# Two product matmuls of every seven-product unit issued as two halves of 128 columns

## The chip, the cores and the metric

The kernel runs on one core of a Trainium2 chip. The metric is the device time of one execution in microseconds (us). A profile shows the core's engines: PE (TensorE, matmuls), PEld (TensorE's weight loads, which run beside its matmuls), DVE (VectorE), ACT (ScalarE), POOL (GpSimd) and SP (SyncE, which here only issues DMAs). A matmul streams its moving operand, column by column, through the array that holds its stationary operand; each matmul here has its own weight load.

## What is computed

A decoder layer on x of 512 tokens by 2048 features, in float32. Cut to what matters:

```python
xn = _rmsnorm(x, norm_w)
proj = jnp.einsum('bsd,de->bse', xn, w_in)          # 2048 -> 14352 columns
q, k, v_m, o_m, z_m, i_pre, f_pre, u_g, v_g, z_g = _split_cols(proj)
...
y_m = hm * jax.nn.sigmoid(o_m) * jax.nn.silu(z_m)   # 8 mLSTM heads, chunks of 128 tokens
...
y_g = u * sv.reshape(B, S, D_G) * jax.nn.silu(z_g)  # 8 groups of causal spatial gating
y = jnp.concatenate([y_m, y_g], axis=-1)
h = x + jnp.einsum('bse,ed->bsd', y, w_out)         # 4096 -> 2048
return _rmsnorm(h, final_norm_w)
```

The two large products, with w_in and with w_out, are most of the work.

## The kernel before

**Products of split operands.** Each float32 operand is split into a rounded high part (ACT casts it) and the rest (DVE subtracts): wh and wl of the weights, xah/xal and xbh/xbl of the input, yah/yal and ybh/ybl of y. A product is then three matmuls, high x high, high x low and low x high, accumulated in PSUM. All are in the rounded 32-bit type.

**Seven products instead of eight.** The projection is done in 28 units of 512 columns (`unit_order`, line 36 on). The first is an ordinary product in 512-column matmuls. Each of the other 27 takes a 2 x 2 block product by seven half-size products (`PRODUCTS`, named q1, q6, q2, q7, q5, q4, q3 in this order), of sums of blocks of x (X[j], made at the start) and of w (sums made by an accumulating DMA, line 151, and by DVE, lines 183 and 184). A unit goes over K in 8 chunks (j = 0 to 7). In each chunk the function `products` issues, for each of the seven, two halves of 128 rows (t = 0, 1) with three matmuls each (a = 0, 1, 2) of 128 x 128 by 256 columns: 42 matmuls a chunk, 336 a unit. They accumulate in seven PSUM banks (`product_banks`) and `combine` adds them up after chunk 7. Outside the four units named qk the x part is stationary and w moves; in qk units (`features`) it is the other way round.

**What follows a unit.** Each unit's activations and so on are queued as small pieces in `bg`, and three are run after each chunk of the next unit. Behind a uz unit some of them hold matmuls: the spatial mixing (`mix`, tile mx, line 455, in full float32) and the transposes of y (`turn`, tile ytg, line 473, 128 columns each), which then stand between products in the second and third chunks of the next unit. After the second unit there are four small products (tile rb_ps, line 260).

**The end.** The g half of w_out follows in ordinary 512-column products (og, lines 853 to 855), with the mLSTM heads' work between them (s, nv, ytm). Then 12 blocks of w_out go by seven products again: 4 column blocks (dq) of 6 chunks (g = 0 to 5), tiles q_m, the same function `products`. The last four blocks are ordinary products (fo, lines 917 to 919), and the final norm.

**Order of the work.** PE, DVE and ACT each run their instructions in program order. Weights come in three buffers of wh and wl and four of the raw wf; chunk n's products are issued after the load of chunk n + 4 and the split of chunk n + 2.

Of the kernel before, what the change touches and what calls it, by code (L numbers as in the profile page):

```python
# [16 lines left out]
P = 128  # L17
D = 2048
S = 512
H = 256  # L20
NT = S // P
KT = D // P
NP = KT // 2
# [24 lines left out]
def hybrid_layer(ctx, tc, xs, x, w_first, w_mid, w_gate, w_out, w_last, par, bif, ws_t, sgu, fin_w, out):  # L48
    nc = tc.nc
# [19 lines left out]
    def half(name):  # L69
        return temp(name)[:, 0:S].rearrange("p (a b) -> p a b", a=2)  # L70
# [64 lines left out]
    raws, splits = {}, {}  # L135

    def load(n):
        if n >= NCH or n in raws:
            return
        kind, src = chunks[n]  # L140
        t = wp.tile([P, 5 * H], F32, tag="wf", name=f"wf{n}", bufs=4)
        raws[n] = t
        if kind == "std":
            if n == 0:
                for kk in range(2):
                    nc.sync.dma_start(t[:, kk * S:(kk + 1) * S], src[:, kk * S:(kk + 1) * S])
            else:
                nc.sync.dma_start(t[:, 0:1024], src)
        else:
            nc.sync.dma_start(t, src)  # L150
            nc.gpsimd.dma_start(t[:, 3 * H:5 * H], t[:, H:3 * H], accum_op=ALU.add)  # L151
# [10 lines left out]
    def split(n):  # L162
        if n >= NCH or n in splits:
            return
        kind = chunks[n][0]
        t = raws[n]
        raws[n] = None
        if kind == "std":
            if n >= NF0 + 2:
                h = xb.tile([P, 2, S], F32R, tag="xb", name=f"fh{n}")  # L170
                l = xb.tile([P, 2, S], F32R, tag="xb", name=f"fl{n}")
            else:
                h, l = (wp.tile([P, WS], F32R, tag=tag, name=f"{tag}{n}", bufs=bufs)[
                    :, OFF:OFF + 1024].rearrange("p (a b) -> p a b", a=2) for tag, bufs in (("wh", 3), ("wl", 3)))
            f = t[:, 0:1024].rearrange("p (a b) -> p a b", a=2)
            nc.scalar.copy(h, f)  # L176
            nc.vector.tensor_tensor(l, f, h.bitcast(F32), op=ALU.subtract)  # L177
            splits[n] = (h, l)
            return
        h = wp.tile([P, WS], F32R, tag="wh", name=f"wh{n}", bufs=3)  # L180
        l = wp.tile([P, WS], F32R, tag="wl", name=f"wl{n}", bufs=3)
        e = wp.tile([P, 2 * H], F32, tag="we", name=f"we{n}", bufs=1)
        nc.vector.tensor_tensor(e[:, 0:H], t[:, 3 * H:4 * H], t[:, 2 * H:3 * H], op=ALU.add)  # L183
        nc.vector.tensor_tensor(e[:, H:2 * H], e[:, 0:H], t[:, 0:H], op=ALU.add)  # L184
        for f, c in ((t, slice(0, 5 * H)), (e, slice(5 * H, WS))):
            nc.scalar.copy(h[:, c], f)  # L186
            nc.vector.tensor_tensor(l[:, c], f, h[:, c].bitcast(F32), op=ALU.subtract)  # L187
        splits[n] = tuple(v.rearrange("p (a b) -> p a b", a=7) for v in (h, l))


    xr, X, A21 = {}, {}, {}
# [478 lines left out]
    Y = {}  # L670

    def load_y(kind, g):
        yh, yl = (xb.tile([P, 2, S], F32R, tag="xb", name=f"y{kind}{c}{g}") for c in "hl")
        for f in range(2):
            t = temp(f"yr{kind}{g}_{f}")[:, 0:S]
            nc.sync.dma_start(t, y_dram[(kind, g)][:, f, :])
            nc.scalar.copy(yh[:, f, :], t)
            nc.vector.tensor_tensor(yl[:, f, :], t, yh[:, f, :].bitcast(F32), op=ALU.subtract)
        Y[(kind, g)] = (yh, yl)
# [32 lines left out]
    def run_bg(k):  # L712
        while k > 0 and bg:
            bg.popleft()()
            k -= 1
# [22 lines left out]
    for j in range(NP):  # L738
        n = j
# [13 lines left out]
        wh, wl = splits.pop(n)  # L753
        blocks = ((X[j][0], A21[j]), (X[j][1], X[j][2]))
        if j == 0:
            for kk in range(2):
                for xp, w in ((0, wh), (1, wh), (0, wl)):
                    for q in range(4):
                        cs = slice((q % 2) * P, (q % 2 + 1) * P)
                        nc.tensor.matmul(acc[q], lhsT=blocks[kk][q // 2][xp][:, cs], rhs=w[:, kk, :],  # L760
                                         start=(kk == 0 and xp == 0 and w is wh), stop=False)
# [9 lines left out]
    c0 = [[half(f"e0_{a}{g}") for g in range(2)] for a in range(2)]  # L771
# [9 lines left out]
    def product_banks(un):  # L781
        return {name: (pp if p < 4 else pm).tile([P, S], F32, tag="p" if p < 4 else "m", name=f"{name}_{un}")
                for p, (name, _, _) in enumerate(PRODUCTS)}

    def products(q, xj, wh, wl, opening, closing, features):
        for name, xsl, wsl in PRODUCTS:
            xh, xl = xj[xsl]
            ps = q[name]
            for t in range(2):
                o = ps[:, t * H:(t + 1) * H]  # L790
                cs = slice(t * P, (t + 1) * P)
                first, last = opening and t == 0, closing and t == 1
                if features:
                    ops = ((wh[:, wsl, cs], xh), (wh[:, wsl, cs], xl), (wl[:, wsl, cs], xh))
                else:
                    ops = ((xh[:, cs], wh[:, wsl, :]), (xh[:, cs], wl[:, wsl, :]), (xl[:, cs], wh[:, wsl, :]))
                for a, (st_, mv_) in enumerate(ops):
                    nc.tensor.matmul(o, lhsT=st_, rhs=mv_, start=(first and a == 0), stop=(last and a == 2),  # L798
                                     skip_group_check=True)

    for un in range(1, NA):
        kind, i = order[un]
        q = product_banks(un)
        for j in range(NP):
            n = un * NP + j
            load(n + 4)
            split(n + 2)
            products(q, X[j], *splits.pop(n), j == 0, j == NP - 1, kind == "qk")
            if j == NP - 1:
                c = combine(un, q)  # L810
                AFTER[kind](i, c)
            if un == NA - 1 and j >= 1:
                load_y("g", j - 1)
            run_bg(3)
# [20 lines left out]
    for m, (kind, dq, g) in enumerate(b_chunks):  # L835
        n = NB0 + m
        load(n + 4)
        split(n + 2)
        wh, wl = splits.pop(n)
        if kind == "g":  # L840
            yh, yl = Y[(kind, g)]
            if g == 0:
                acc = [pp.tile([P, S], F32, tag="p", name=f"og{dq}_{q}") for q in range(4)]
                res = []
                for q in range(4):
                    t = temp(f"xr{dq}_{q}")
                    nc.sync.dma_start(t, x[q * P:(q + 1) * P, dq * S:(dq + 1) * S])
                    res.append(t)
            for q in range(4):
                cs = slice(q * P, (q + 1) * P)  # L850
                for kk in range(2):
                    st, sp_ = (g == 0 and kk == 0), (g == NH - 1 and kk == 1)
                    nc.tensor.matmul(acc[q], lhsT=yh[:, kk, cs], rhs=wh[:, kk, :], start=st, stop=False)  # L853
                    nc.tensor.matmul(acc[q], lhsT=yh[:, kk, cs], rhs=wl[:, kk, :], start=False, stop=False)  # L854
                    nc.tensor.matmul(acc[q], lhsT=yl[:, kk, cs], rhs=wh[:, kk, :], start=False, stop=sp_)  # L855
                if g == NH - 1:
                    t = res[q]
                    nc.vector.tensor_tensor(t, t, acc[q], op=ALU.add)
                    nc.sync.dma_start(acc_dram[:, q, dq * S:(dq + 1) * S], t)
            run_bg(6)  # L860
            if dq == 3:
                flush(("m", g))
                if g < 6:
                    sums_y(g)
                else:
                    load_y("m", g)
        else:
            if g == 0:
                q = product_banks(f"m{dq}")
                res = {}  # L870
                for a in range(2):
                    for b in range(2):
                        t = half(f"xc{dq}_{a}{b}")
                        nc.sync.dma_start(t, block(acc_dram, a, b, dq))
                        res[(a, b)] = t
            products(q, Y[("m", g)], wh, wl, g == 0, g == 5, False)
            if g == 5:
                c = combine(f"m{dq}", q)
                for a in range(2):
                    for b in range(2):  # L880
                        t = res[(a, b)]
                        nc.vector.tensor_tensor(t, t, c[a][b], op=ALU.add)
                        if dq < 3:
                            nc.sync.dma_start(block(acc_dram, a, b, dq), t)
                        else:
                            for k in range(2):
                                xacc[(2 * a + k, dq, b)] = t[:, k, :]
    for tt in range(NT):
        for dq in range(3):
            t = row(f"xacc{tt}_{dq}")[:, 0:S]  # L890
# [8 lines left out]
    for a in range(4):  # L899
        t = temp(f"fw{a}")  # L900
# [4 lines left out]
    for tt in range(NT):  # L905
# [4 lines left out]
        for dq in range(4):  # L910
            ps = pp.tile([P, S], F32, tag="p", name=f"fo{tt}_{dq}")
# [110 lines left out]
```

## Time and profile before

| | us |
|---|---|
| median of 3 runs | 1561.7 |
| the three runs | 1553.22, 1561.70, 1561.98 |
| the profiled execution | 1571.57 |
| its span, first to last instruction | 1569.9 |

| stretch of the span | us | what runs |
|---|---|---|
| first unit | 0 to 60 | 512-column products, split of x |
| 27 seven-product units | 60 to 1153 | 9,072 matmuls at line 798 |
| g half of w_out, mLSTM heads | 1153 to 1395 | 512-column products |
| seven products of w_out | 1395 to 1514 | 1,008 matmuls at line 798 |
| last blocks, final norm | 1516 to 1570 | 512-column products |

In the timeline of PE a row gives the start and the length in us, the engine, line, operation, output and inputs, the size, how many were merged, and behind it the idle time before it with what ended it. Matmuls overlap: one is 0.28 us long from its start to its modelled end, but the next starts some 0.115 us after it. The distance from start to start is what one costs, and the length is not. In a row of a wait or of the windows x144 means that 144 instructions touch the stretch.

### The profile page before, as it was taken

The page shows a single profiled execution, that of the slowest core. Times are in us where ns is not written, and L with a number is a line of the kernel's source. Part 1 is how long each engine was busy: PE and PEld are TensorE (multiplying, and loading weights), DVE is VectorE, ACT ScalarE, POOL GpSimd, SP SyncE. Part 2 cuts the span into 40 slices and gives each one's busy share as a digit, 9 for nine tenths or more (in the row PEclk, how much of TensorE's full clock was granted, in tenths as well). Part 3 has the DMA queues.
Part 4 walks back from the last instruction along what each step waited for, and adds up shares of the span by engine and source line. Part 5 has one row for each costly group of instructions (what it writes and reads, how often), then busy time and mean ns, then how long its engine had stood idle before and what let it go on. Part 6 is the DMA issues. An engine that isn't in the chain of part 4 may idle for free. (4 is left out here: it accounts for less than half of the span.)

```text
span 1569.9 us, 30095 instructions
## 1 busy us (share of the span) xinstructions
PE 1545.9 (98%) x11864; PEld 1485.4 (95%) x11864; DVE 1183.7 (75%) x1944; ACT 874.6 (56%) x1340; POOL 285.3 (18%) x384
## 2 busy tenths in 40 slices
PE   9999999999999999999999999999999999999997
PEld 7899999999999999999999999999988788889986
DVE  8787767877966876976877977678887665697875
ACT  6665455654654555554655565454776666553333
POOL 1411112211122211121211111111202222011100
PEclk9999999999999999999999999999999999999999
DMA  9777878787788777778787777877964665798962
GB/s 319 210 192 187 228 177 209 185 202 193 213 203 215 188 211 184 210 190 214 192 211 186 200 203 199 212 201 196 277 195 156 206 226 188 238 265 238 277 231 107
DMA packets 118510, 326.99 MB, mean 208 GB/s; under 512 B 13534, under 2 KB 20702, under 8 KB 118369
## 3 DMA queue, kind: packets, MB, share of 16 engines
q1 hardware_dynamic: 77456, 243.30, 48.1%
q0 software_dynamic: 40192, 80.66, 26.7%
q8 instruction: 93, 1.52, 0.4%
q10 hardware_dynamic: 720, 1.11, 0.2%
q14 instruction: 49, 0.39, 0.1%
HBM read 229.37 MB, written 32.74 MB: 167 GB/s over the span
## 5 line engine op out<-in xcount | busy, mean ns | idle before, releaser
L186 ACT CAST wh<-wf 128x1280 fp32r<-128x1280 f32 x240 | 301.9, 1264 | 379.9 <-issue 237.8
L187 DVE TENSOR_TENSOR wl<-wf,wh 128x1280 fp32r<-128x1280 f32 x240 | 356.7, 1488 | 174.3 <-ACT wh L186 174.0
L798 PE MATMUL q<-wh,xbh 128*128 128x256 f32 x1472 | 413.7, 281 | 1.4 <-ACT e L774 1.4
L798 PE MATMUL q<-wl,xbh 128*128 128x256 f32 x1472 | 412.9, 281 | 1.2 <-DVE wl L187 1.2
L798 PE MATMUL q<-wh,xbl 128*128 128x256 f32 x1472 | 412.7, 280 | 0.0
L151 POOL DMA_DIRECT2D wf<-wf x240 | 205.3, 857 | 1010.9 <-DMA wf<-w_mid 243.2
L798 PE MATMUL q<-wh,xah 128*128 128x256 f32 x1104 | 311.8, 282 | 0.0
L798 PE MATMUL q<-wl,xah 128*128 128x256 f32 x1104 | 309.5, 280 | 0.0
L798 PE MATMUL q<-wh,xal 128*128 128x256 f32 x1104 | 309.4, 280 | 0.0
L798 PEld LDWEIGHTS q<-wh,xbh 128*128 128x128 f32 x1472 | 281.1, 191 | 1.8 <-ACT e L774 1.6
L798 PEld LDWEIGHTS q<-wl,xbh 128*128 128x128 f32 x1472 | 276.9, 188 | 1.9 <-DVE wl L187 1.8
L798 PEld LDWEIGHTS q<-wh,xbl 128*128 128x128 f32 x1472 | 276.3, 188 | 0.0
L798 PEld LDWEIGHTS q<-wh,xah 128*128 128x128 f32 x1104 | 210.8, 191 | 0.7 <-ACT e L774 0.2
L798 PEld LDWEIGHTS q<-wl,xah 128*128 128x128 f32 x1104 | 207.7, 188 | 0.1
L798 PEld LDWEIGHTS q<-wh,xal 128*128 128x128 f32 x1104 | 207.2, 188 | 0.0
L186 ACT CAST wh<-we 128x512 fp32r<-128x512 f32 x240 | 148.2, 618 | 89.6 <-DVE we L184 89.2
L187 DVE TENSOR_TENSOR wl<-we,wh 128x512 fp32r<-128x512 f32 x240 | 164.7, 686 | 17.2 <-ACT wh L186 17.2
L183 DVE TENSOR_TENSOR we<-wf 128x256 f32<-128x256 f32 x240 | 101.4, 422 | 20.0 <-issue 9.0
L184 DVE TENSOR_TENSOR we<-we,wf 128x256 f32<-128x256 f32 x240 | 101.4, 423 | 5.4
L853 PE MATMUL og<-wh,ygh 128*128 128x512 f32 x256 | 100.9, 396 | 1.6 <-ACT wh L176 1.6
L854 PE MATMUL og<-wl,ygh 128*128 128x512 f32 x256 | 101.5, 397 | 0.1
L855 PE MATMUL og<-wh,ygl 128*128 128x512 f32 x256 | 101.3, 396 | 0.0
(284 smaller groups left out, 2865.9 us busy)
## 6 DMA issues: line engine op xcount, KB each, us to landing
wf<-w_mid SPq DMA_DIRECT2D x216, 640.0 KB, 4.7
wf<-wf POOLq DMA_DIRECT2D x240, 256.0 KB, 5.2
wf<-w_out_p SPq DMA_DIRECT2D x40, 512.0 KB, 4.1
wf<-w_last SPq DMA_DIRECT2D x24, 640.0 KB, 5.7
xr<-xs SPq DMA_DIRECT2D x16, 256.0 KB, 6.1
xt<-x SPq DMA_DIRECT2D x8, 512.0 KB, 7.5
ozd<-e SPq DMA_DIRECT2D x16, 256.0 KB, 2.6
ygd<-yfg SPq DMA_DIRECT2D x16, 256.0 KB, 4.5
```

The source lines that it names most:

```text
L151: nc.gpsimd.dma_start(t[:, 3 * H:5 * H], t[:, H:3 * H], accum_op=ALU.add)
L183: nc.vector.tensor_tensor(e[:, 0:H], t[:, 3 * H:4 * H], t[:, 2 * H:3 * H], op=ALU.add)
L184: nc.vector.tensor_tensor(e[:, H:2 * H], e[:, 0:H], t[:, 0:H], op=ALU.add)
L186: nc.scalar.copy(h[:, c], f)
L187: nc.vector.tensor_tensor(l[:, c], f, h[:, c].bitcast(F32), op=ALU.subtract)
L798: nc.tensor.matmul(o, lhsT=st_, rhs=mv_, start=(first and a == 0), stop=(last and a == 2), skip_group_check=True)
L853: nc.tensor.matmul(acc[q], lhsT=yh[:, kk, cs], rhs=wh[:, kk, :], start=st, stop=False)
L854: nc.tensor.matmul(acc[q], lhsT=yh[:, kk, cs], rhs=wl[:, kk, :], start=False, stop=False)
L855: nc.tensor.matmul(acc[q], lhsT=yl[:, kk, cs], rhs=wh[:, kk, :], start=False, stop=sp_)
```

## The change

`products` takes one more argument, `cut`, the name of a product with t and a. The one matmul that it names is issued as two matmuls of 128 columns with the same stationary operand, into the two halves of the same 256 PSUM columns. In the 27 units that is in the first chunk (j = 0) the first of the last three matmuls (q3, t = 1, a = 0), and in the fifth (j = 4) the fourth (q1, t = 1, a = 0); in the last stage the fourth of the second and the fourth chunk of each column block (g = 1 and 3). What is computed stays the same.

```diff
-    def products(q, xj, wh, wl, opening, closing, features):
+    def products(q, xj, wh, wl, opening, closing, features, cut=None):
         for name, xsl, wsl in PRODUCTS:
             xh, xl = xj[xsl]
             ps = q[name]
             for t in range(2):
-                o = ps[:, t * H:(t + 1) * H]
                 cs = slice(t * P, (t + 1) * P)
...
                 for a, (st_, mv_) in enumerate(ops):
-                    nc.tensor.matmul(o, lhsT=st_, rhs=mv_, start=(first and a == 0), stop=(last and a == 2),
-                                     skip_group_check=True)
+                    parts = (0, P, H) if (name, t, a) == cut else (0, H)
+                    for c0, c1 in zip(parts, parts[1:]):
+                        nc.tensor.matmul(ps[:, t * H + c0:t * H + c1], lhsT=st_, rhs=mv_[:, c0:c1],
+                                         start=(first and a == 0), stop=(last and a == 2), skip_group_check=True)
...
-            products(q, X[j], *splits.pop(n), j == 0, j == NP - 1, kind == "qk")
+            cut = {0: ("q3", 1, 0), 4: ("q1", 1, 0)}.get(j)
+            products(q, X[j], *splits.pop(n), j == 0, j == NP - 1, kind == "qk", cut)
...
-            products(q, Y[("m", g)], wh, wl, g == 0, g == 5, False)
+            products(q, Y[("m", g)], wh, wl, g == 0, g == 5, False, ("q1", 1, 0) if g in (1, 3) else None)
```

On the other engines the instructions and their order stay. On PE, the end of the first chunk of the second unit before (q_1_763 is q3's bank, wh_617 and wl_618 the weights, xbh_302 and xbl_303 the x part; x2 means two alike):

```order
L798 MATMUL q_1_763<-wh_617,xbh_302 128x256
L798 MATMUL q_1_763<-wl_618,xbh_302 128x256
L798 MATMUL q_1_763<-wh_617,xbl_303 128x256
L798 MATMUL q_1_763<-wh_617,xbh_302 128x256
L798 MATMUL q_1_763<-wl_618,xbh_302 128x256
L798 MATMUL q_1_763<-wh_617,xbl_303 128x256
L260 MATMUL rb_ps<-diag,ones 128x128 x2
```

The same place now:

```order
L799 MATMUL q_1_763<-wh_617,xbh_302 128x256
L799 MATMUL q_1_763<-wl_618,xbh_302 128x256
L799 MATMUL q_1_763<-wh_617,xbl_303 128x256
L799 MATMUL q_1_763<-wh_617,xbh_302 128x128 x2
L799 MATMUL q_1_763<-wl_618,xbh_302 128x256
L799 MATMUL q_1_763<-wh_617,xbl_303 128x256
L260 MATMUL rb_ps<-diag,ones 128x128 x4
```

The fourth matmul has become two of 128 columns. The four small products behind it now stand together, where they were parted by three products of the next chunk.

## The prediction

> **What bounds the kernel now.** I read the page first, then the PE waits, then the PE timeline matmul by matmul, because a PE that is busy all the time can still run at different paces.
>
> ```profile
> span 1569.9 us, 30095 instructions
> PE 1545.9 (98%) x11864; PEld 1485.4 (95%) x11864; DVE 1183.7 (75%) x1944; ACT 874.6 (56%) x1340; POOL 285.3 (18%) x384
> ...
> PE ytm L473 <- DVE oz L639: 2.5, 1, 2.5
> ```
>
> PE is busy for 98% of the span, and the longest single wait of PE on anything is 2.5 us. So time can hardly be won by hiding something; it is the spacing of the matmuls that counts. Of the 11,864 matmul records 10,080 are the products at L798 (27 units of 8 chunks of 42, and 4 of 6 chunks of 42). The spacing comes from the timeline: the first and last row of two stretches without interruption, 172 records and 153 records.
>
> ```profile
> 309.80 0.28 PE L798 MATMUL q<-wh,xbl 128*128 128x256 f32 x1
> ...
> 329.94 0.28 PE L798 MATMUL q<-wh,xal 128*128 128x256 f32 x1
> ...
> 388.75 0.28 PE L798 MATMUL q<-wh,xah 128*128 128x256 f32 x1
> ...
> 405.97 0.28 PE L798 MATMUL q<-wh,xbl 128*128 128x256 f32 x1
> ```
>
> 171 steps in 20.14 us are 117.8 ns each; 152 steps in 17.22 us are 113.3 ns. The same instruction on the same shapes has two paces, 4.5 ns apart, and each pace lasts for hundreds of matmuls. Whole units show it too (columns: stretch, its length, then busy time and count of PE, PEld, DVE, ACT, POOL, clock, DMA share, GB/s):
>
> ```profile
> 388.40:426.96 38.56, 38.37 (x338) 38.17 (x337) 36.67 (x60) 21.53 (x26) 6.41 (x9) 1.00 0.79 214
> 548.01:587.59 39.58, 39.58 (x339) 39.58 (x338) 28.49 (x42) 23.41 (x29) 7.65 (x9) 1.00 0.80 207
> 1073.62:1112.19 38.57, 38.38 (x338) 38.18 (x337) 36.15 (x58) 21.53 (x26) 6.32 (x8) 1.00 0.77 211
> 1450.00:1490.00 40.00, 40.00 (x342) 39.98 (x341) 34.12 (x53) 15.52 (x18) 7.59 (x9) 1.00 0.96 265
> ```
>
> The first and third line are the only two units that run nearly whole at the fast pace; the second is an ordinary one at the slow pace. The granted clock is 1.00 in all, so it is no clock state. Following the timeline through all units, I count about 1,070 fast products, nearly all in these two units, the beginning of the units behind them, and short pieces of some 43 matmuls in four others. About 9,000 are slow. If all became fast, 9,000 x 4.5 ns = 40 us would go.
>
> What switches the pace? Interruptions of the stream:
>
> ```profile
> 152.09 0.28 PE L798 MATMUL q<-wh,xbl 128*128 128x256 f32 x1
> 152.56 1.03 PE L455 MATMUL mx<-e,ws 128*128 128x256 f32 x4
> 154.13 0.28 PE L798 MATMUL q<-wh,xbh 128*128 128x256 f32 x1
> ...
> 155.95 0.28 PE L798 MATMUL q<-wl,xbh 128*128 128x256 f32 x1
> ...
> 159.10 0.60 PE L473 MATMUL ytg<-ident,e 128*128 128x128 f32 x4
> 160.12 0.28 PE L798 MATMUL q<-wh,xal 128*128 128x256 f32 x1
> 160.80 0.28 PE L798 MATMUL q<-wh,xbl 128*128 128x256 f32 x1
> 161.14 0.66 PE L473 MATMUL ytg<-ident,e 128*128 128x128 f32 x4
> 161.76 0.28 PE L798 MATMUL q<-wl,xah 128*128 128x256 f32 x1
> 162.93 0.28 PE L798 MATMUL q<-wh,xbl 128*128 128x256 f32 x1
> ```
>
> Before the mixing products (mx) the pace is slow; after them it is fast (154.13 to 155.95, 16 steps, 114 ns), still fast after the first transposes (160.12 to 160.80, 6 steps, 113 ns), and slow after the second (161.76 to 162.93, 10 steps, 117 ns), where it stays to the next interruption. The same sequence repeats behind four other uz units. So the pace is a lock between the stream of weight loads and the stream of matmuls; a disturbance shifts one against the other, and they settle again in one lock or the other.
>
> **The change, part by part.** It removes nothing and moves no work between engines; 62 matmuls (27 units x 2, 4 x 2 in the last stage) become two halves each, so PE and PEld get 62 instructions more. Each pair is a disturbance in the sense above, one every 168 matmuls.
>
> *Price of a cut.* No row shows such a half. Nearest are the transposes, 128 columns each with a weight load of their own:
>
> ```profile
> L473 PE MATMUL ytg<-ident,e 128*128 128x128 f32 x64 | 10.0, 279 | 0.4
> L260 PE MATMUL rb_ps<-diag,ones 128*128 128x128 f32 x8 | 1.3, 287 | 0.2 <-DVE diag L259 0.2
> ```
>
> Four of them take 0.60 us from the first start to the last end (159.10); less the 0.28 us of the last, three steps are 0.32 us, 108 ns a step, though half the columns are streamed. A pair then costs 216 ns where one matmul cost 113 or 118: +100 ns. Settling again, as behind the interruptions above, I put at 10 to 15 ns. So 62 x 0.115 = +7.1 us, all on the path, because PE has no slack. The bounds: at the low end a half streams in half of 113 ns and its load hides, +0. At the high end a half runs like the plain f32 matmuls of rb_ps, whose four matmuls leave eight records, two passes of about 110 ns each: a pair 440 ns, +330 ns, 62 x 0.33 = +20 us. The operands here are the rounded type of the products, which pass once, and the transposes pass once too; so I take +7.1.
>
> The Trainium skill, "TensorE: Matmul & The Clock Gate", speaks against the change in "LDWEIGHTS (loading the stationary operand)": a load takes its 128 columns over 1.2, 106.7 ns, whatever the matmul streams. By it the estimate for a pair is 213 ns, +100 over a fast product, 62 x 0.10 = 6.2 us; the transposes' 108 ns agree.
>
> *Which lock follows a cut.* This decides, and no row shows it. For fast: all ten mixings outside the qk units were followed by the fast pace, and in two of four cases the mere change from a qk unit to the next one. For slow: the second transposes, five times of five. Of the kinds of disturbance in these units somewhat over half end fast. A cut has one advantage over the others: its geometry is always the same, without a wait on another engine, so from the fast lock it gives always the same answer. If that answer is "fast", the fast lock absorbs: once in, each later cut keeps it, and the slow lock is left at one of the next cuts. I take this case.
>
> *What it is then worth.* 23 of the 27 units aren't qk: 7,728 products, less the 1,070 already fast, 6,660. Slow remain those ahead of the first cut (39), ahead of it behind two qk units (78), between the second transposes and the fifth chunk in five units (5 x 35), and behind stalls (80): about 370. 6,290 x 4.5 ns = -28.0 us. In the qk units and the last stage no fast lock is seen at all; two long stretches there, 156 and 172 records:
>
> ```profile
> 366.73 0.28 PE L798 MATMUL q<-xbh,wl 128*128 128x256 f32 x1
> ...
> 384.98 0.28 PE L798 MATMUL q<-xal,wh 128*128 128x256 f32 x1
> ...
> 1399.80 0.28 PE L798 MATMUL q_m<-wh,ybl 128*128 128x256 f32 x1
> ...
> 1419.94 0.28 PE L798 MATMUL q_m<-wh,ybl 128*128 128x256 f32 x1
> ```
>
> Both are 117.8 ns. For the qk units (streams exchanged) I count nothing, at most 1,344 x 4.5 = -6 us. The last stage has the operands' roles of the others, so I count half of 960 x 4.5 = 4.3: -2; not all, since its DMA share is already 0.96 in the row 1450:1490, and 4% more pace would bring it to 1.0.
>
> *What becomes late next.* In the two fast units PE stalls once each, behind a split:
>
> ```profile
> 408.13 0.28 PE L798 MATMUL q<-wh,xbh 128*128 128x256 f32 x1
> 408.60 0.39 PE L798 MATMUL q<-wl,xbh 128*128 128x256 f32 x1 [0.19 <-DVE wl L187]
> ```
>
> A step of 0.47 us and another of 0.22 instead of 0.113, about 0.46 us in all: DVE is busy 36.67 of 38.56 us there, with the convolutions of the qk unit before. Two more units follow a qk unit: +0.9. Elsewhere DVE has a quarter of its time free (28.49 of 39.58), which covers 4%.
>
> *Sum:* -28.0 - 2 + 0.9 + 7.1 = -22.0 us, against the profiled execution's 1571.6 (its span of 1569.9 and 1.7 around it): 1549.6. The timed runs are all shorter, 1553.2 to 1562.0, the median 1561.7, by 9.9. If they were shorter because more of their products were fast already, nothing of this comes off again, and 1549.6 stands; if the recording costs it, all comes off, 1539.7. I take the middle, **1544 us**, 1.1% under the median.
>
> **Rivals.**
> - *The cuts lead to the slow lock.* Speaks for it: 9,000 of 10,080 products fell into it. Then each cut ends a fast stretch; of the 1,070 fast products most are lost, 1,000 x 4.5 = +4.5, with +7.1: 1583 on the profiled time, 1573 if the recording costs 9.9. It decides when a cut met in the fast lock is followed by 117.8 ns. Where only some cuts do so, gain and price cancel: 1550 to 1565.
> - *The halves cost as much as plain f32.* +20 instead of +7 with the lock won: 1557. For it: the kernel widens a 128-column product elsewhere to 256 columns, as if narrow ones were dear.
> - *There is only one pace per width, and a cut is free.* Two halves of 57 ns hide their loads, and no lock shifts: 1562, no change. Against it: the two paces above. The Trainium skill, the same page, "Back-to-back issue gap", gives this: one gap of N over 2.4 plus 2.5 ns, 109.2 for 256 columns and 55.8 for 128, so 62 cuts cost an estimated 0.15 us; the trace differs, 117.8 or 113.3 and never 109.2.
> - *The supply can't follow.* DVE or DMA hold fast units to the 38.57 us seen, not 38.08 (336 x 113.3): 19 more units x 0.49 = +9: 1553.
>
> **How the numbers follow.** The fast lock prevails: 0.55, with 1535 to 1553 as its own range. Mixed, supply-bound or dear halves: 0.17, 1550 to 1565. No lock and free: 0.05. Slow lock: 0.23, 1565 to 1583. About 1%, 16 us, is what a measurement of this kernel can tell from no change. Faster than 1546: 0.40, nearly all from the first case. Slower than 1577: 0.12, from the slow lock. Same: 0.48, the upper part of the first case among it. The range, 1534 to 1572, leaves out a few hundredths below and the upper half of the slow lock.
>
> **What would show it.** Right: units of 38.1 to 38.3 us in the windows, spacing of 113.3 ns behind the cuts at the end of the first and at the start of the fifth chunk, and the fast pace kept across unit boundaries. The cut's price: from the start of a first half to the next full product 0.21 to 0.23 us; 0.44 means dear halves, 0.12 free ones. Wrong: spacing of 117.8 ns behind a cut that was met at 113.3. What breaks the forecast is the lock, which I could only count, not derive.

## The result and the profile after

| | before | changed |
|---|---|---|
| median of 8 runs, us | 1561.91 | 1547.72 |
| lowest and highest | 1553.22 to 1571.33 | 1540.38 to 1551.11 |
| profiled execution | 1571.57 | 1548.42 |
| slow steps (over 115.5 ns) among its products | 8,934 | 1,067 |

The ratio is 0.9896 with a 95% interval of 0.9871 to 0.992: about 1.0% faster, and 14 us between the medians. The last row of the table counts, in the PE timeline, every step from the start of one full product to the start of the next product (or of its first half, where that is cut) that is under 130 ns, and parts them at 115.5 ns. One run of e9 below took 2540.01 us at a granted clock of 0.557, where all others had 0.99 and more, and is left out of its median and ratio.

From the page of the changed kernel:

```profile
span 1546.7 us, 30196 instructions
...
PE 1521.3 (98%) x11926; PEld 1459.0 (94%) x11926; DVE 1182.0 (76%) x1944; ACT 873.5 (56%) x1340; POOL 282.0 (18%) x384
```

62 instructions more on PE and on PEld, and PE still busy for 98%: nothing was hidden, the same work is paced differently. Two units in the windows (columns as before), the fourth seven-product unit and the qk unit behind an oz unit:

```profile
182.87:221.20 38.33, 38.33 (x340) 38.33 (x339) 27.44 (x40) 19.26 (x26) 7.53 (x9) 1.00 0.83 220
1014.60:1052.91 38.31, 38.31 (x340) 38.31 (x339) 28.61 (x42) 22.05 (x28) 6.87 (x8) 1.00 0.79 210
```

A unit without an interruption took 39.58 us and takes 38.33. That is 38.08, as for a unit of e4 below that is fast throughout without a cut (336 steps of 113.3 ns), and 0.25 for two cuts. Now a cut that the stream met at the fast pace, in the PE timeline of the changed kernel (the two halves are merged into one row, x2):

```profile
305.75 0.28 PE L799 MATMUL q<-wh,xbh 128*128 128x256 f32 x1
305.86 0.28 PE L799 MATMUL q<-wl,xbh 128*128 128x256 f32 x1
305.98 0.28 PE L799 MATMUL q<-wh,xbl 128*128 128x256 f32 x1
306.09 0.33 PE L799 MATMUL q<-wh,xbh 128*128 128x128 f32 x2
306.26 0.33 PE L799 MATMUL q<-wl,xbh 128*128 128x256 f32 x1
306.43 0.28 PE L799 MATMUL q<-wh,xbl 128*128 128x256 f32 x1
306.55 0.28 PE L799 MATMUL q<-wh,xah 128*128 128x256 f32 x1
...
306.90 0.28 PE L799 MATMUL q<-wh,xah 128*128 128x256 f32 x1
...
307.12 0.28 PE L799 MATMUL q<-wh,xal 128*128 128x256 f32 x1
```

The steps before are 0.11 to 0.12; the pair and the product behind it take 0.17 each, then three steps of 0.12 settle, and from 306.90 on it is 0.11 again. From 306.09 to 307.12 are 1.03 us where eight fast steps are 0.91: the cut costs 0.12. And one that was met at the slow pace:

```profile
1096.74 0.28 PE L799 MATMUL q<-wh,xal 128*128 128x256 f32 x1
...
1097.09 0.28 PE L799 MATMUL q<-wh,xbl 128*128 128x256 f32 x1
1097.21 0.33 PE L799 MATMUL q<-wh,xbh 128*128 128x128 f32 x2
...
1097.67 0.28 PE L799 MATMUL q<-wh,xah 128*128 128x256 f32 x1
...
1098.23 0.28 PE L799 MATMUL q<-wh,xal 128*128 128x256 f32 x1
```

Three steps of 0.35 us together before (117 ns), five of 0.56 us behind (112 ns): the cut moved the stream into the fast lock.

**Where the time went**, by the starts of the first and last products in the two timelines. The units take 1069.9 us instead of 1092.6, 22.7 less: by the counts some 6,900 products fewer are slow there, -30.7 at 4.45 ns each, against +6.7 for 54 cuts; the remaining +1.3 I put down to stalls and settling. The first unit ended 1.0 later, the heads' stage took 1.3 less and the tail behind the last stage 1.4 more, and in all three nothing was changed. There the clock differed. Short stretches run at a granted clock of 0.50, before and now:

```profile
1166.80:1170.20 3.40, 3.36 (x8) 2.69 (x9) 2.70 (x4) 2.51 (x3) 0.00 (x0) 0.50 0.88 321
1228.30:1231.60 3.30, 3.24 (x9) 2.56 (x10) 3.30 (x9) 2.66 (x9) 1.36 (x6) 0.50 0.50 151
```

```profile
1205.50:1208.80 3.30, 3.23 (x10) 2.54 (x10) 3.30 (x9) 2.66 (x9) 1.36 (x6) 0.50 0.52 161
1502.40:1505.80 3.40, 3.40 (x10) 2.65 (x9) 3.40 (x7) 2.17 (x6) 0.00 (x0) 0.50 0.00 0
```

In them a 512-column product steps by 427 ns, otherwise by some 227. In the heads' stage ten og products did so before and four now (-1.2 us), in the tail none and seven fo products (+1.4), in the first unit five and eight (+0.6; a wait for ACT of 0.52 is the rest). The changed kernel's traced execution has 19 such steps in all, some 3.8 us, and the same kernel in e6 none, so no effect of the change is shown in them. The last stage, before and now:

```profile
1394.89:1514.10 119.21, 119.04 (x1009) 118.72 (x1007) 90.44 (x131) 46.38 (x54) 16.87 (x20) 1.00 0.92 265
```

```profile
1371.87:1489.50 117.63, 116.85 (x1017) 115.71 (x1015) 90.70 (x132) 47.37 (x55) 16.84 (x20) 1.00 0.93 267
```

It became 1.6 us shorter though nearly all its products turned fast (1,008 x 4.5 ns = 4.5, less 1.0 for eight cuts), since PE now stands still in it six times; with the slower step behind each that costs 2.3 us, where it cost 0.5. The longest of these waits, and what stands ahead of it:

```profile
1456.56 1.27 ACT L186 CAST wh<-wf 128x1280 fp32r<-128x1280 f32 x1 [1.86 <-DMA wf<-wf]
1457.86 1.49 DVE L187 TENSOR_TENSOR wl<-wf,wh 128x1280 fp32r<-128x1280 f32 x1 [0.49 <-ACT wh L186]
1459.87 0.68 DVE L372 TENSOR_TENSOR em<-em,q_m 128x512 f32<-128x512 f32 x1
1460.61 0.39 PE L799 MATMUL q_m<-wh,ybh 128*128 128x256 f32 x1 [0.29 <-DVE em L372]
```

PE waits until DVE has added up a bank of the block before; DVE was held up by the split, the split by ACT's cast, and the cast by a DMA. Altogether +1.0 - 22.7 - 1.3 - 1.6 + 1.4 = -23.2, the difference of the spans.

### The profile page after: what moved, and what is told of

Its sections match the earlier page's. It is cut to its first block, busy times and chain, and to the rows that moved or that the text cites. A ratio compares the mean times of both kernels' runs of the same rounds, so it can differ in the third digit from the quotient of the medians.

```text
span 1546.7 us, 30196 instructions
## 1 busy us (share of the span) xinstructions
PE 1521.3 (98%) x11926; PEld 1459.0 (94%) x11926; DVE 1182.0 (76%) x1944; ACT 873.5 (56%) x1340; POOL 282.0 (18%) x384
## 4 chain that ended last, share of the span: by engine, by line
PE 74%; DVE 13%; DMA 6%; issue 3%; ACT 3%; POOL 1%; SPq 0%; ACTq 0%; POOLq 0%; DVEq 0%
PE q L799 55%; PE q_m L799 4%; DVE wl L187 3%; PE og L857 2%; PE og L856 2%; PE og L855 2%; DMA wf<-wf 2%; DVE qc L520 1%; PE mx L455 1%; PE fo L920 1%; ACT wh L186 1%; PE fo L921 1%; DVE wl L177 1%; PE fo L919 1%; DMA xr<-x 1%
## 5 line engine op out<-in xcount | busy, mean ns | idle before, releaser
L799 PE MATMUL q<-wh,xbh 128*128 128x256 f32 (+1 forms) x1495 | 409.0, 276 | 1.4 <-ACT e L774 1.4
L799 PE MATMUL q<-wh,xbl 128*128 128x256 f32 x1472 | 406.6, 276 | 0.0
L799 PE MATMUL q<-wh,xah 128*128 128x256 f32 (+1 forms) x1127 | 307.6, 276 | 1.2 <-DVE e L373 0.7
L799 PE MATMUL q<-wh,xal 128*128 128x256 f32 x1104 | 305.0, 276 | 0.0
```

Source lines behind the costliest of these rows:

```text
L799: nc.tensor.matmul(ps[:, t * H + c0:t * H + c1], lhsT=st_, rhs=mv_[:, c0:c1], start=(first and a == 0), stop=(last and a == 2), skip_group ...
```

## The experiments

Theory A is that of the prediction: a cut shifts weight loads against matmuls, and they settle in the fast lock and stay. Theory B, the rival, is that each cut speeds what stands next to it, so that gain goes with the number of cuts. In all tables the slow steps are those of the profiled execution, and the ratio is to runs of the kernel before on the same chip.

**Half of the cuts, and four times as many.** The line with a minus is the change's; the three that take its place are those of e1, e2 and e3. The last stage's cuts follow it: at g = 1 alone, at g = 3 alone, at every g.

```diff
-            cut = {0: ("q3", 1, 0), 4: ("q1", 1, 0)}.get(j)
+            cut = {0: ("q3", 1, 0)}.get(j)
+            cut = {4: ("q1", 1, 0)}.get(j)
+            cut = ("q3", 1, 0) if j == 0 else ("q1", 1, 0)
```

> Only the cut at the end of the first chunk of the 27 units stays, and the one at g = 1 of the last stage: 31 cuts instead of 62. Theory A (a cut shifts weight loads against matmuls, they settle in the fast lock of 113.3 ns and stay there until another interruption): the units that no interruption parts stay fast between cuts, so little is lost but the stretches behind transposes and stalls that settle slow, some 5 units x 200 products x 4.5 ns = +4 us, against 31 x 0.127 = -3.9 us for the cuts saved: 1545 to 1552 us. Theory B (every cut speeds only the products next to it, so that the gain goes with the number of cuts): half of the gain goes, 1555 us.

> Only the cut at the start of the fifth chunk of the 27 units stays, and the one at g = 3 of the last stage: 31 cuts. Theory A (lock): the first half of the second unit stays slow (168 x 4.5 ns = 0.8 us), and the first chunks behind qk units (4 x 170 x 4.5 = 3 us); all else stays fast, since this cut stands behind the interruptions of the second to fourth chunk; 3.9 us of cuts saved: 1544 to 1551 us. Theory B (gain by number of cuts): 1555 us.

> A cut in each of the 8 chunks of the 27 units and each of the 24 of the last stage: 240 instead of 62. Theory A (lock, and 0.127 us a cut, 0.113 in qk units): the products are as fast as with 62 cuts, and 178 x 0.125 = +22 us come on top: 1570 us, the gain all given back. Theory B (gain by number of cuts): faster than with 62. If halves were free: 1546 us.

| run | cuts | median, us | ratio, interval | span | slow steps |
|---|---|---|---|---|---|
| e1, first chunk only | 31 | 1550.08 | 0.9932, 0.9908 to 0.9956 | 1547.8 | 1,668 |
| e2, fifth chunk only | 31 | 1546.71 | 0.9914, 0.9883 to 0.9945 | 1544.1 | 1,305 |
| e3, every chunk | 240 | 1570.85 | 1.006, 1.0031 to 1.009 | 1568.4 | 1,087 |

Theory B falls with e3: four times the cuts, the same share of fast products as in the changed kernel, and slower than before. One unit of e3 in its windows:

```profile
185.37:224.46 39.09, 39.09 (x347) 39.09 (x345) 27.44 (x40) 19.25 (x26) 6.78 (x8) 1.00 0.84 216
```

39.09 is 38.08 and 1.01 for eight cuts, 0.126 each. Over the whole kernel 178 more cuts lengthened the span by 21.7 us against the changed kernel's profiled execution, 0.122 each. The first-chunk cuts alone (e1) leave slow what settles slow behind them: three units stayed so from the fifth chunk to their end. The fifth-chunk cuts alone (e2) lose the four half units behind qk units, and are as good as both.

**Few cuts.**

```diff
+            cut = ("q3", 1, 0) if un in (1, 9, 15, 21, 26) and j == 0 else None
+            cut = ("q1", 1, 0) if un in (3, 5, 10, 16, 22) and j == 4 else cut
...
+            products(q, Y[("m", g)], wh, wl, g == 0, g == 5, False, ("q1", 1, 0) if dq == 0 and g == 1 else None)
```

> 11 cuts in all, where the fast lock has to be won: end of the first chunk of the second unit and of the four behind qk units, fifth chunk of the five other units behind uz units, and g = 1 of the first column block of the last stage. Theory A (lock, kept without help until an interruption): 51 x 0.125 = -6.4 us for the cuts saved, +2 to +4 for stretches lost behind single stalls: 1541 to 1546 us, faster than with 62 cuts. Theory B (gain by number of cuts): 1559 us, hardly faster than before.

Median 1546.84, ratio 0.9909 (0.988 to 0.9938) with 11 cuts: as the changed kernel with 62, not faster, and a little over the 1541 to 1546 expected. Its span was 1542.8 with 2,662 slow steps, and without one of the 427 ns steps. Three units of e4:

```profile
103.16:142.73 39.57, 39.57 (x338) 39.57 (x337) 28.48 (x42) 23.39 (x29) 6.79 (x8) 1.00 0.79 199
184.42:222.50 38.08, 38.08 (x339) 38.08 (x337) 27.45 (x40) 19.27 (x26) 6.79 (x8) 1.00 0.83 220
1091.89:1131.46 39.57, 39.57 (x338) 39.57 (x337) 35.09 (x55) 29.46 (x41) 4.99 (x8) 1.00 0.76 238
```

The middle one holds no cut at all and runs wholly at the fast pace, won one unit earlier: the lock is kept across a unit's end. The first came slow out of the unit before, the last after a stall in the unit before it. The unit ahead of the first had a cut; why it lost the lock all the same stands in the timeline:

```profile
66.35 0.33 PE L799 MATMUL q<-wh,xbh 128*128 128x128 f32 x2
...
66.81 0.61 PE L260 MATMUL rb_ps<-diag,ones 128*128 128x128 f32 x4
67.98 0.38 PE L260 MATMUL rb_ps<-diag,ones 128*128 128x128 f32 x1 [0.57 <-DVE diag L259]
```

The four small products, in full float32 and with a wait, come straight behind the cut and disturb the stream again; it then stayed slow for some 710 products, until the mixing behind the next uz unit. In the changed kernel the same four products stand behind the same cut: in its first trace the pace behind them was 113 ns, in e6, the same program, 118. So the kind of an interruption doesn't fix how it ends.

**Cuts placed by what the traces showed**, beside the changed kernel once more.

```diff
+PLACED = ({(1, 2), (27, 2)} | {(un, j) for un in (9, 15, 21, 26) for j in (1, 5)}
+          | {(un, 4) for un in (3, 5, 6, 8, 10, 12, 14, 16, 18, 20, 22)})
...
+            cut = ("q1", 1, 0) if (un, j) in PLACED else None
...
+            products(q, Y[("m", g)], wh, wl, g == 0, g == 5, False, ("q1", 1, 0) if g == 1 else None)
```

> 25 cuts, each at the start of a chunk that stands behind an interruption after which some execution settled slow: third chunk of the second and of the last unit, first and sixth chunk of the four units behind qk units, fifth chunk of the units behind uz and vv units, and g = 1 of each column block. Theory A (lock): 62 - 25 = 37 cuts less save 4.5 us against the changed kernel, and no slow stretch lasts longer than there: 1540 to 1545 us. Theory B (more cuts, more gain): 1555 us.

> The changed kernel once more beside the one with 25 cuts: 1545 to 1550 us by every theory; it is the yardstick.

| run | cuts | median, us | ratio, interval | span | slow steps |
|---|---|---|---|---|---|
| e5, placed | 25 | 1547.97 | 0.9892, 0.986 to 0.9925 | 1540.4 | 945 |
| e6, changed kernel | 62 | 1550.80 | 0.9897, 0.9871 to 0.9923 | 1545.9 | 1,510 |

The placed cuts have the shorter median, but it is over the 1540 to 1545 expected, and the intervals lie on each other; this is no proof that they are better. The runs of e5 spread from 1542 to 1558, perhaps because with fewer cuts a stall that ends slow costs more; only the fastest of them was traced.

**Uneven parts.** The change as it is, with the cut at 64 of 256 columns in the first chunk and at 192 in the fifth.

```diff
-                    parts = (0, P, H) if (name, t, a) == cut else (0, H)
+                    parts = (0, cut[3], H) if cut and (name, t, a) == cut[:3] else (0, H)
```

> The 62 cuts of the change, but at 64 of the 256 columns in the first chunk (and g = 1) and at 192 in the fifth (and g = 3). If any disturbance without a wait leads to the fast lock, both kinds are followed by 113.3 ns and the time stays within 1545 to 1552 us. If the lock depends on the size of the shift, at least one of the two is followed by 117.8 ns from the fast lock, and the time goes to 1555 to 1575 us. The price of a cut: 0.113 to 0.127 us for both, if each part waits for a weight load of its own.

One run, 1555.34 us (the kernel before on this chip: median 1567.8), 3,292 slow steps. From the fast lock both kinds led back to the fast one, nearly always, and at the price of equal halves. But four whole units, the fourth and the eleventh to thirteenth of those with seven products, that had turned slow kept the slow lock, though each had its two cuts. In the fourth:

```profile
188.83 0.28 PE L799 MATMUL q<-wh,xal 128*128 128x256 f32 x1
...
189.19 0.28 PE L799 MATMUL q<-wh,xbl 128*128 128x256 f32 x1
189.31 0.36 PE L799 MATMUL q<-wh,xbh 128*128 128x64 f32 x2
189.51 0.30 PE L799 MATMUL q<-wl,xbh 128*128 128x256 f32 x1
189.65 0.28 PE L799 MATMUL q<-wh,xbl 128*128 128x256 f32 x1
...
190.35 0.28 PE L799 MATMUL q<-wh,xal 128*128 128x256 f32 x1
```

117 to 120 ns before, six steps of 117 ns behind. In the units that are not qk, of 14 such cuts met slow 11 ended slow. Equal halves outside the qk units do better: over the nine traces other than e3's that have them, 67 were met slow and followed by ten undisturbed products, and all 67 ended fast; of 182 met fast, 179 ended fast, and the other three, in e8, had a short stall right behind them. e3 adds 33 met slow and 148 met fast, and all ended fast. So it isn't any disturbance that helps: outside the qk units the place of the cut in its product matters, and the middle is a good one. The sign that was expected, a cut that loses the fast lock, did not show there; the uneven cuts failed to win it.

**Cuts in qk units.** There the changed kernel's cut, met slow, stays slow (three of three, and again in e6). It isn't always so: in e5 one stayed slow too, but in e2 one and in e3 three that were met slow ended fast.

```diff
+            cut = {0: ("q3", 1, 0, 128), 4: ("q1", 1, 0, 128)}.get(j)
+            if kind == "qk":
+                cut = {3: ("q1", 1, 1, 128), 4: ("q1", 1, 2, 128), 5: ("q1", 1, 0, 64), 6: ("q1", 1, 0, 192)}.get(j)
```

> The change as it is, except for the qk units: there a cut of the second matmul of a product (fourth chunk), of the third (fifth chunk), of the first at 64 columns (sixth) and at 192 (seventh). In the changed kernel the qk units behind uz units stay slow behind the mixing, and the cut of the first matmul at 128 leaves them slow. If another cut wins the fast lock there, three units gain up to 200 x 4.5 ns each, 2.7 us in all, less 6 cuts more in them and in the fourth qk unit (0.8 us): 1544 to 1549 us; if none does, 1548 to 1552 us.

One run, 1555.44 us with 2,106 slow steps, later than expected. Of the four forms only the one at 64 columns won the fast lock, in all three units behind uz units; the one at 192, a chunk later, lost it in all four. First the one, then the other:

```profile
368.58 0.28 PE L799 MATMUL q<-xbh,wl 128*128 128x256 f32 x1
...
369.05 0.36 PE L799 MATMUL q<-xah,wh 128*128 128x64 f32 x2
...
369.39 0.28 PE L799 MATMUL q<-xah,wl 128*128 128x256 f32 x1
...
370.07 0.28 PE L799 MATMUL q<-xbh,wl 128*128 128x256 f32 x1
...
373.36 0.28 PE L799 MATMUL q<-xbl,wh 128*128 128x256 f32 x1
...
373.92 0.30 PE L799 MATMUL q<-xah,wh 128*128 128x192 f32 x2
...
374.27 0.28 PE L799 MATMUL q<-xah,wl 128*128 128x256 f32 x1
...
374.98 0.28 PE L799 MATMUL q<-xbh,wl 128*128 128x256 f32 x1
```

From 369.39 six steps take 0.68 us (113 ns); from 374.27 six take 0.71 (118 ns). Here is the rival of the slow lock, observed: a cut from which the stream comes out slow.

> The 25 placed cuts, those of the three qk units behind uz units (fifth chunk) now at 64 columns instead of 128, the only form that won the fast lock in these units. In the run with 25 cuts two of the three came to the fast lock by themselves and one stayed slow for 200 products, so the gain is 0 to 2.7 us in an execution: 1540 to 1548 us, and 1 to 6 us under the changed kernel. If the 64-column cut loses the fast lock where it meets it, 1 to 3 us over the run with 25 cuts.

This was the 25 placed cuts with that 64-column form in three qk units. Median 1549.94 of five runs, over the 1540 to 1548 expected; ratio 0.9891 (0.9863 to 0.9918), 2,370 slow steps. The 64-column cuts failed three times of three: all three met the slow lock and left it slow. In e8 two other cuts had come before in the same unit. So the form alone doesn't decide either; what stands before it matters too, perhaps by the moment at which the cut is met.

**Where the tiles lie.** No cut at all, only an empty tile in front made 64 bytes larger: in e10 (the first line with a plus) all weight tiles lie 64 bytes further, in e11 (the second) the x tiles and what follows them.

```diff
-GAP_X, GAP_W = 24, 112
+GAP_X, GAP_W = 24, 128
+GAP_X, GAP_W = 40, 112
```

> The kernel before, without any cut; only the empty tile ahead of the weight buffers is 64 bytes larger in each partition, so that all weight tiles lie 64 bytes further against the x tiles. If the two paces come from where the two streams lie in memory, at least one of 117.8 and 113.3 ns changes, or the share of the fast one changes much. If they come from timing alone, both paces stay and the time is within 1553 to 1572 us.

> The kernel before, without any cut; the empty tile ahead of the x tiles is 64 bytes larger, so that x and the weights behind it are moved together against the tiles ahead of them. Same reading: other paces if the place matters, the same two and 1553 to 1572 us if it is timing alone.

One run each: 1596.82 and 1550.80 us, beside 1562 to 1574 of the kernel before on this chip. The first and last of 169 products in a stretch of e10, and one unit of it:

```profile
309.73 0.28 PE L798 MATMUL q<-wh,xbh 128*128 128x256 f32 x1
...
329.89 0.28 PE L798 MATMUL q<-wh,xbh 128*128 128x256 f32 x1
```

```profile
559.01:599.33 40.32, 40.32 (x339) 40.32 (x338) 29.29 (x43) 23.41 (x29) 7.01 (x9) 1.00 0.74 202
```

168 steps in 20.16 us are 120.0 ns, a third pace; of 10,001 counted steps 12 were fast. In e11 two units:

```profile
181.85:219.93 38.08, 38.08 (x338) 38.08 (x337) 27.45 (x40) 19.27 (x26) 6.79 (x8) 1.00 0.86 224
538.58:578.16 39.58, 39.58 (x338) 39.58 (x337) 28.49 (x42) 23.40 (x29) 6.79 (x8) 1.00 0.76 200
```

The two known paces, but here the fast one is usual without a single cut (2,564 slow steps). So timing alone isn't it: in e10 both known paces are gone, and which paces there are hangs on where the tiles lie. e11 alone shows less, since it is one run and moves x and the weights together; the kernel before, unmoved, reached 1546.79 us in one of its runs beside e12, on another chip.

> The x tiles 64 bytes further as in the run before, which alone was as fast as the changed kernel, and nine cuts: at the start of the sixth chunk of three units behind vv units, of the first chunk of the unit behind the last qk unit, of the fifth chunk of the last unit, and g = 1 of each column block, the places behind which the run with x moved had its long slow stretches (some 1,750 products). If x moved makes the fast lock the usual one and a cut keeps doing what it did, 1,200 to 1,700 of these become fast, -5 to -7.5 us, +1.1 for the cuts: 1543 to 1548 us, 1.1 to 1.5% under the kernel before of the same chip. If a cut answers otherwise with x moved, or the single run was a lucky one, 1550 to 1560 us.

```diff
-GAP_X, GAP_W = 24, 112
+GAP_X, GAP_W = 40, 112
+PLACED = {(6, 5), (12, 5), (18, 5), (26, 0), (27, 4)}
...
+            cut = ("q1", 1, 0) if (un, j) in PLACED else None
...
+            products(q, Y[("m", g)], wh, wl, g == 0, g == 5, False, ("q1", 1, 0) if g == 1 else None)
```

Median 1544.05 of 12 runs, ratio 0.9918 (0.989 to 0.9947) on a chip where the kernel before took 1556.79; span 1541.9, 1,149 slow steps. All nine cuts left the stream fast. The time is as expected, the gain isn't: 0.8% instead of 1.1 to 1.5. It is the lowest median of the study, but its ratio isn't under the changed kernel's: no version was shown to beat the change.

## Why the prediction was right

**The two paces, and that cuts switch them: shown.** Behind nearly every cut the pace was the fast one, from either side, and e4 and e11 have whole units at 38.08 us without a cut in them. What I had counted, not derived, that the answer of a cut from the fast lock would be "fast", held; e7 and e8 show that it need not have: parts of 192 columns in a qk unit do the opposite.

**The shift of weight loads against matmuls: not shown.** A product and the next weight load, in the kernel before, first at the slow pace, then at the fast one:

```profile
319.93 0.28 PE L798 MATMUL q<-wl,xah 128*128 128x256 f32 x1
319.93 0.19 PEld L798 LDWEIGHTS q<-wh,xal 128*128 128x128 f32 x1
...
394.87 0.28 PE L798 MATMUL q<-wh,xah 128*128 128x256 f32 x1
394.87 0.19 PEld L798 LDWEIGHTS q<-wl,xah 128*128 128x128 f32 x1
```

The two streams stand alike at both paces: in the undisturbed products of this trace the next load starts 2 to 5 ns behind a product's start. What differs is the time from the start of a product's own load to the product's start, 110 ns at the fast pace and nearly always 114 to 117 at the slow one. So the paces last until something disturbs the stream, as the prediction has it, but what it is that is shifted the records don't say; "lock" here names the behaviour and not a known cause.

**The price of a cut: right, a little low.** Of the extra time of a cut 0.115 us were forecast. Measured at the undisturbed cuts are 0.127, 0.113 in qk units, where nothing has to settle: one more weight-load slot, as the transposes had it, and 13 ns of settling. 62 of them are about 7.8 us, not 7.1. The dear halves, +0.33, and the free ones fell. Only my reading aid was off: the extra time doesn't stand between the first half and the next product but half of it in the step behind that product, 0.17 and 0.17.

**The gain: as forecast outside the qk units, and some more in them.** In the 23 other units 6,310 products turned fast, beside 6,290 forecast (which at 4.5 ns are 28.3 us; the sum has 28.0). The qk units added 590. I had counted nothing for them, because no fast lock was seen in them; entered fast, they stay fast, up to the mixing where there is one (the unit at 1014.60 to its end).

**The last stage: -2 forecast, -1.6 measured.** Nearly all its products turned fast, not half, and the stalls behind DVE took 1.8 us of that back. So the supply rival was right for this stage in this execution, though the DMA share rose only from 0.92 to 0.93. In e5, with four cuts there, it didn't hold:

```profile
1370.55:1486.04 115.49, 115.32 (x1013) 114.85 (x1011) 91.08 (x132) 47.52 (x55) 16.87 (x20) 1.00 0.95 278
```

That is 3.7 us under the kernel before, with next to no stall.

**The step that was wrong: half of the 9.9 us between the profiled execution and the median.** The sum against the profiled execution's own time gave 1549.6, and the changed kernel's profiled execution took 1548.42. I then took 5 us off in case the recording costs time. It doesn't show: the changed kernel's profiled execution lies 0.7 from its median, and the kernel before reached 1571.33 in another run. Its runs spread by 18 us, which 4,000 products changing lock would explain, but only one of its executions was traced; the spread of the changed kernel is 11. So 1544 was 3.7 under the 1547.72 measured, and the likeliest case came out with the gain at the bound that I had set for a measurable one.

**What stays open.** Why a shift ends fast or slow was not derived. e10 shows that the paces depend on 64 bytes of placement, not which port or bank of memory the streams meet in. The Trainium skill, "TensorE: Matmul & The Clock Gate", says under "Step-by-step: what each phase is for" that PE has two independent read ports, so that loading the next weights takes no read bandwidth from the running matmul. No run here settles whether that holds: the same instructions took 113.3, 117.8 or 120.0 ns a step, the last with the weight tiles 64 bytes further, but that it is bandwidth that the two streams take from each other isn't shown.

## What to carry to other kernels

Where an engine is busy for 98%, look at the distance from start to start of equal instructions in several stretches: if there are two paces, the difference times the count is the most that can be won, here 40 us; the 62 cuts won 14 between the medians. Before shifting the stream by cuts, try where the operands lie: one run with a constant changed by 64 bytes was as fast here as 62 cuts (it may have been a lucky one), and one run with the other constant changed was 30 us slower than the kernel before. And put a cut behind what disturbs the stream, not ahead of it, and no more of them than needed, since each costs a weight load.

## What I had not expected of the hardware

- A stream of equal matmuls keeps one of two paces for hundreds of them, up to a thousand: 113.3 or 117.8 ns a step at a granted clock of 1.00, until something interrupts it.
- A placement 64 bytes further gave a third pace, 120.0 ns, and left the fast one in 12 of 10,001 steps, in the one run that was made.
- A matmul of 128 columns with a weight load of its own costs as much as one of 256 (0.113 us more for a pair), and parts of 64 and 192 columns cost the same as two of 128, so the price goes with the load and not with the columns.
- Stretches of some 3.4 us at a granted clock of 0.50 stand at other places in each execution: there a 512-column product steps by 427 ns instead of 227, and an execution has 0 (e4, e6) to 28 (e12) such steps.
